# Two gate/up groups of each FFN as seven block products, interleaved with plain groups, and weights in blocks of 2048 columns

## The chip, the core and the metric

The kernel runs on one core of one Trainium2 chip. The metric is the device time of one execution in microseconds (us). TensorE (PE) multiplies, VectorE (DVE) and ScalarE (ACT) do the elementwise work, GpSimd (POOL) takes the powers in the norms, and SyncE (SP) issues the DMA transfers.

## The reference: what is computed

A two-layer decoder trunk over 256 tokens of width 1024. Each layer is FFN, mixer, FFN, so that there are four FFNs of width 2816; the mixers are a causal pooling and a dilated window attention. Every sublayer has an RMS norm on its input and one on its output. The part that the change is about:

```python
def swiglu(h, w_gate, w_up, w_down):
    return (jax.nn.silu(h @ w_gate) * (h @ w_up)) @ w_down
...
f = swiglu(rms_norm(h, g[0]), ffn_w_gate[layer, 0], ffn_w_up[layer, 0], ffn_w_down[layer, 0])
h = h + 0.5 * rms_norm(f, g[1])
```

## The kernel before, in words

The 256 tokens are two halves `i` of 128. A norm gives the activations, and `transposed` turns them with PE transposes into `aT`, as a rounded part (`aT[:, 0]`) and a rest (`aT[:, 1]`). The weights are treated the same way. `load_unit` (L83) loads a unit of 128x1024 fp32 (512 KB) into `raw` (four buffers) on SP's queue; ACT casts it to its rounded part (L92), DVE subtracts that from the unit for the rest (L93), and both stand in `hl` (eight buffers of one unit). Each product of a weight with an activation is three matmuls: rounded x rounded, rounded activation x rest of the weight, rest of the activation x rounded weight (`proj_mm` L106, `row_mm` L121). So ACT's cast has to be there for the first matmul with a unit, and DVE's subtraction for the second.

In an FFN (`ffn` L211) the 2816 hidden columns are five groups of 512 (`c` = 0 to 4) and one of 256 that holds gate and up beside each other (NG). A group's gate is 4 units, and so is its up; each unit serves both token halves. One group is 2 (gate, up) x 2 (halves) x 8 (blocks of 128 of the width) x 3 = 96 matmuls with 512 columns; an FFN has 5 x 96 + 48 = 528 of them. `gate` (L216) takes the silu on ACT, `up` (L221) multiplies on DVE, and `turn` (L226) transposes a half's product (four PE transposes, one ACT cast, one DVE subtraction) into `h2`, which the down projection reads: 22 units, 12 matmuls each. The last six units of the down projection (`TAIL`) are held back, so that half 0 is completed first: its post-norm, residual, next pre-norm and transposes (`Bound`, L306) run beside the last 36 matmuls of half 1. In the next FFN half 0 then has 48 matmuls (8 units of group 0) to be done while half 1 goes through the same norms.

Nobody writes out the order on the engines: a scheduler puts the instructions of each engine in a row when the kernel is built, by the order of the program and the buffers. Each engine then works its row strictly in that order, and so does SP's queue. Two things in the order matter below: a transfer into a buffer can be issued only when the last reader of that buffer is done, and whatever stands behind a waiting instruction on its engine waits too.

Of the kernel before, what the change touches and what calls it, by code (L numbers as in the profile page):

```python
# [11 lines left out]
F32 = mybir.dt.float32  # L12
F32R = mybir.dt.float32r
# [6 lines left out]
P = 128  # L20
S = 256
# [6 lines left out]
TAIL = 6  # L28
WARM = 64
CAST = 1024  # L30
# [17 lines left out]
def trunk_kernel(ctx: ExitStack, tc: tile.TileContext, x, pos, gains, pscale, ws, wq, invf, amask, pmat, icnt, out):  # L48
# [6 lines left out]
    s8p = ctx.enter_context(tc.tile_pool(name="s8p", bufs=6))  # L55
# [25 lines left out]
    unit_no = [0]  # L81
    last = {}

    def load_unit():
        u = unit_no[0]
        unit_no[0] += 1
        raw = rawp.tile([P, 1024], F32, tag="raw", name=f"raw{u}")
        last["dma"] = nc.sync.dma_start(raw, ws[u])
        hl = hlp.tile([P, 2, 1024], F32R, tag="hl", name=f"hl{u}")
        for c in range(0, 1024, CAST):  # L90
            w = slice(c, c + CAST)
            nc.scalar.copy(hl[:, 0, w], raw[:, w])  # L92
            last["dve"] = nc.vector.tensor_sub(hl[:, 1, w], raw[:, w], hl[:, 0, w])  # L93
        return hl

    def load_q_unit(u):
        raw = rawp.tile([P, 1024], F32, tag="raw", name=f"rawq{u}")
        nc.sync.dma_start(raw[:, :768], wq[u])
        hl = hlp.tile([P, 2, 1024], F32R, tag="hl", name=f"hlq{u}")
        nc.scalar.copy(hl[:, 0, :768], raw[:, :768])  # L100
        nc.vector.tensor_sub(hl[:, 1, :768], raw[:, :768], hl[:, 0, :768])
        return hl
# [72 lines left out]
    def transposed(i, src, dst, name):  # L175

        for b in range(2):
# [6 lines left out]
            nc.vector.tensor_sub(d[:, 1], tp, d[:, 0])  # L184

# [25 lines left out]
    def ffn(n, aT, boundary, middle=None):  # L211

        h2 = [s8p.tile([P, 2, 4, S], F32R, tag="s8", name=f"h2_{n}_{c}") for c in range(NG + 1)]
        act, prod = {}, {}

        def gate(c, i, g):  # L216
            w = g.shape[-1]
            act[c, i] = sc2.tile([P, 512], F32, tag="w2", name=f"s_{n}_{c}{i}")
            nc.scalar.activation(act[c, i][:, :w], g, AF.Silu)

        def up(c, i, u):  # L221
            w = u.shape[-1]
            prod[c, i] = sc2.tile([P, 512], F32, tag="w2", name=f"m_{n}_{c}{i}")
            nc.vector.tensor_mul(prod[c, i][:, :w], u, act[c, i][:, :w])
# [10 lines left out]
        def both(ps, units, c=None):  # L235

            for q in range(4):
                for i in range(2):
                    proj_mm(ps[i], aT, i, units, 512, only=q)
                if c is not None and q < 2:  # L240
                    turn(c, q)

        units = [load_unit() for _ in range(8 - len(first_units))]
        units, first_units[:] = first_units + units, []
# [11 lines left out]
        for c in range(1, NG):  # L256
            units = [load_unit() for _ in range(4)]
            ps = [gup.tile([P, 512], F32, tag="gu", name=f"g_{n}_{c}{i}") for i in range(2)]
            both(ps, units, c - 1)
            for i in range(2):  # L260
                gate(c, i, ps[i])
            units = [load_unit() for _ in range(4)]
            ps = acc_pair(f"u{n}{c}")
            both(ps, units)
            for i in range(2):
                up(c, i, ps[i])
            if c == 2 and middle is not None:
                middle()
        units = [load_unit() for _ in range(4)]
        ps = [gup.tile([P, 512], F32, tag="gu", name=f"g_{n}_{NG}{i}") for i in range(2)]  # L270
        both(ps, units, NG - 1)
        for i in range(2):
            gate(NG, i, ps[i][:, 0:256])
            up(NG, i, ps[i][:, 256:512])

# [7 lines left out]
        for c in range(NF - TAIL):  # L283
            u = load_unit()
            down(c, 0, u)
            down(c, 1, u)
# [477 lines left out]
```

## Time and profile before

| what | value |
|---|---|
| median of 3 runs | 992.54 us (991.7 to 993.55) |
| profiled execution, its own time | 995.63 us |
| its span, first to last instruction | 993.7 us |
| mean granted TensorE clock | 0.992 |
| PE busy | 975.3 us (98%) |
| DVE busy | 575.0 us (58%) |
| ACT busy | 484.4 us (49%) |
| DMA, over the span | 180.38 MB, mean 182 GB/s |

Terms are made against the profiled execution (995.63 us), which is 3.09 us above the median and 1.9 us longer than its span. In rows of groups, the last fields are the busy time in us, the mean duration in ns, and the idle time of the engine ahead of the group with what ended it. A busy PE may be waiting inside: the rate of PE is read from the starts of its instructions.

### The profile page before, as it was taken

The numbers are of one execution on the slowest core, as the hardware profiler recorded it, in microseconds if no ns is written. First come the engines' busy times: TensorE is split into PE (matmuls) and PEld (weight loads), VectorE is DVE, ScalarE is ACT, GpSimd is POOL, SyncE is SP. The second block draws the span as 40 slices with busy tenths as digits, with TensorE's granted clock in tenths as the row PEclk, the third lists the DMA queues.
The fourth block names the chain that finished last, engine by engine and source line by source line (L and its number), as shares of the span: only waits on it lengthen the run. The fifth ranks groups of instructions, "written<-read, shape, count | busy, mean of one in ns | idle before, by whom it ended". The sixth has DMA issues, their size and how long they took to land.

```text
span 993.7 us, 12240 instructions
## 1 busy us (share of the span) xinstructions
PE 975.3 (98%) x4664; PEld 810.1 (82%) x4664; DVE 575.0 (58%) x725; ACT 484.4 (49%) x660; POOL 23.2 (2%) x34
## 2 busy tenths in 40 slices
PE   7999999999999999999999999999999999999997
PEld 6888888878788888877888888788898888888886
DVE  5665554578765555447665554685556466555542
ACT  5644443365564444346554443554455565444431
POOL 0000000010100000000000000100000000000000
PEclk8999999999999999999999999999999899999999
DMA  6855655666465575535755756474533137556531
GB/s 224 292 185 188 228 186 189 203 193 213 145 218 185 190 233 180 191 127 174 263 188 171 231 179 197 150 244 154 152 124 128 44 100 260 191 181 203 188 127 42
DMA packets 53722, 180.38 MB, mean 182 GB/s; under 512 B 7265, under 2 KB 7265, under 8 KB 53665
## 3 DMA queue, kind: packets, MB, share of 16 engines
q1 hardware_dynamic: 53584, 179.35, 55.4%
q8 instruction: 36, 0.59, 0.2%
q0 software_dynamic: 80, 0.26, 0.1%
q14 instruction: 22, 0.17, 0.1%
HBM read 178.54 MB, written 1.05 MB: 181 GB/s over the span
## 4 chain that ended last, share of the span: by engine, by line
PE 88%; DVE 4%; issue 3%; ACT 2%; POOL 2%; DMA 1%; SPq 0%; POOLq 0%; DVEq 0%; ACTq 0%
PE g L105 22%; PE acc_d L105 21%; PE acc_u L105 19%; PE acc_b L105 7%; PE vp L105 3%; PE qp L105 3%; PE kp L105 3%; PE htp L230 2%; PE ob L105 1%; PE acc_w L105 1%; PE acc_o L105 1%; DVE h L171 1%; DVE hl L93 1%; ACT hl L92 1%; PE sc L105 1%
## 5 line engine op out<-in xcount | busy, mean ns | idle before, releaser
L93 DVE TENSOR_TENSOR hl<-raw,hl 128x1024 fp32r<-128x1024 f32 x310 | 378.5, 1224 | 298.8 <-ACT hl L92 296.7
L92 ACT CAST hl<-raw 128x1024 fp32r<-128x1024 f32 x310 | 325.5, 1051 | 338.5 <-PE acc_d L105 101.1
L105 PE MATMUL acc_d<-hl,h 128*128 128x512 f32 x1056 | 242.9, 390 | 0.0
L105 PEld LDWEIGHTS acc_d<-hl,h 128*128 128x128 f32 x1056 | 197.4, 188 | 40.7
L105 PE MATMUL g<-hl,aT_m 128*128 128x512 f32 x480 | 116.1, 394 | 0.0
L105 PEld LDWEIGHTS g<-hl,aT_m 128*128 128x128 f32 x480 | 88.6, 188 | 17.8
L105 PE MATMUL acc_u<-hl,aT_m 128*128 128x512 f32 x384 | 88.3, 389 | 0.0
L105 PEld LDWEIGHTS acc_u<-hl,aT_m 128*128 128x128 f32 x384 | 72.1, 188 | 15.0
L105 PE MATMUL acc_u<-hl,aT_f 128*128 128x512 f32 x288 | 67.2, 390 | 0.0
L105 PEld LDWEIGHTS acc_u<-hl,aT_f 128*128 128x128 f32 x288 | 53.8, 188 | 11.5 <-DVE aT_f L184 0.5
L105 PE MATMUL g<-hl,aT_f 128*128 128x512 f32 x240 | 58.7, 395 | 0.0
L105 PE MATMUL g<-hl,aT_x 128*128 128x512 f32 x240 | 58.1, 394 | 0.0
L105 PEld LDWEIGHTS g<-hl,aT_x 128*128 128x128 f32 x240 | 44.3, 188 | 8.9
L105 PEld LDWEIGHTS g<-hl,aT_f 128*128 128x128 f32 x240 | 44.2, 188 | 8.7
L105 PE MATMUL acc_b<-hl,aT_m 128*128 128x512 f32 x192 | 45.3, 392 | 0.1
L105 PE MATMUL acc_u<-hl,aT_x 128*128 128x512 f32 x192 | 44.2, 389 | 0.0
L105 PEld LDWEIGHTS acc_u<-hl,aT_x 128*128 128x128 f32 x192 | 36.0, 188 | 7.5
L105 PEld LDWEIGHTS acc_b<-hl,aT_m 128*128 128x128 f32 x192 | 35.7, 188 | 7.8 <-DVE aT_m L184 0.5
L105 PE MATMUL qp<-hlq,aT_f 128*128 128x384 f32 x192 | 39.1, 346 | 0.0
L105 PE MATMUL kp<-hl,aT_hk 128*128 128x512 f32 x144 | 34.5, 394 | 0.0
L105 PEld LDWEIGHTS qp<-hlq,aT_f 128*128 128x128 f32 x192 | 32.7, 188 | 0.4
L105 PE MATMUL vp<-hl,aT_hk 128*128 128x512 f32 x144 | 33.1, 390 | 0.0
(158 smaller groups left out, 831.3 us busy)
## 6 DMA issues: line engine op xcount, KB each, us to landing
raw<-in_ws SPq DMA_DIRECT2D x310, 512.0 KB, 3.5
rawq<-in_wq SPq DMA_DIRECT2D x16, 384.0 KB, 3.6
gain_post<-in_gains SPq DMA_DIRECT2D x14, 256.0 KB, 4.6
gain_pre<-in_gains SPq DMA_DIRECT2D x12, 256.0 KB, 5.6
rawpm<-in_pmat SPq DMA_DIRECT2D x2, 512.0 KB, 4.7
out_dram<-h SPq DMA_DIRECT2D x4, 256.0 KB, 2.1
h<-in_x SPq DMA_DIRECT2D x2, 256.0 KB, 3.0
h<-in_x SPq DMA_DIRECT2D x1, 512.0 KB, 8.5
```

Source lines behind the costliest of these rows:

```text
L92: nc.scalar.copy(hl[:, 0, w], raw[:, w])
L93: last["dve"] = nc.vector.tensor_sub(hl[:, 1, w], raw[:, w], hl[:, 0, w])
L105: nc.tensor.matmul(o, l, r, start=start, stop=stop)
L171: nc.vector.scalar_tensor_tensor(h[i][:, c], y[:, c], rs, h[i][:, c], op0=ALU.mult, op1=ALU.add)
L230: nc.tensor.transpose(tp[:, k], prod[c, i][:, k * P : (k + 1) * P], ident)
```

## The change

Groups 1 and 2 of an FFN become one `pair`, and so do groups 3 and 4. In a pair, the first group's gate and up are computed together. The activations, by token half and half of the width, are a 2x2 matrix A of blocks of 128x512. The weights are a 2x2 matrix of blocks of 512x512: X and W are the gate's columns in the first and the second half of the width, Y and Z the up's. Instead of eight products of a block of A with a block of weights, 12 matmuls each, there are seven: with X, X+Y, X+Y+Z, Z, Y+Z, W and X+Y+Z+W as weights, and with four sums of blocks of A, `S`, that `Sums` makes once after the norm (three ACT copies, four DVE sums, four ACT casts and four DVE subtractions of 128x512). The pair's second group is computed as before, its blocks placed between the seven products. So a pair has 84 + 96 = 180 matmuls instead of 192.

The weights come in blocks of 128x2048 (1 MB, two units). X and Y have buffers of their own (`xyp`, two), every other block goes through `rawp` (now three), and the halves through `hlp` (now three blocks, six units). The sums of weights are made in place by DVE (`add`); as each sum is a new weight, it is cast and subtracted anew: 7 + 4 wide casts and subtractions in a pair instead of 16 narrow ones (of the size of 8 wide ones), and 4 wide adds. X+Y+Z+W needs W. In `rawp`'s turn of three, W is the third block after Z, so it is loaded into Z's buffer. The norm of K and V moves from the middle of the third FFN (`middle`) to just ahead of its down projection (`late`).

The core of the diff:

```diff
-    rawp = ctx.enter_context(tc.tile_pool(name="rawp", bufs=4))
-    hlp = ctx.enter_context(tc.tile_pool(name="hlp", bufs=8))
+    rawp = ctx.enter_context(tc.tile_pool(name="rawp", bufs=3))
+    xyp = ctx.enter_context(tc.tile_pool(name="xyp", bufs=2))
+    hlp = ctx.enter_context(tc.tile_pool(name="hlp", bufs=3))
...
+    def load_raw(parts=1, pool=rawp, tag="raw"):
...
+        raw = pool.tile([P, 2, 1024], F32, tag=tag, name=f"{tag}{b}")
+        flat = raw.rearrange("p u n -> p (u n)")
+        for k in range(parts):
+            w = slice(k * (2048 // parts), (k + 1) * (2048 // parts))
+            last["dma"] = nc.sync.dma_start(flat[:, w], ws[b, :, w])
+        return raw
+
+    def halves(raw, parts=1, n=1024):
+        hl = hlp.tile([P, 2, 2, 1024], F32R, tag="hl", name="hl")
+        for k in range(parts):
+            u = slice(k * (2 // parts), (k + 1) * (2 // parts))
+            nc.scalar.copy(hl[:, 0, u, :n], raw[:, u, :n])
+            last["dve"] = nc.vector.tensor_sub(hl[:, 1, u, :n], raw[:, u, :n], hl[:, 0, u, :n])
+        return [hl[:, :, j] for j in range(2)]
...
+    class Sums:
...
+        def add_half(self, i, b, tp):
+            a = self.a
+            if (i, b) != (1, 1):
+                a[i, b] = self.tmp(f"{i}{b}")
+                nc.scalar.copy(a[i, b], tp)
+            if (i, b) == (1, 0):
+                s3 = self.tmp("s")
+                nc.vector.tensor_sub(s3, a[0, 0], tp)
+                self.parts(2, s3)
+            if (i, b) == (1, 1):
+                nc.vector.tensor_sub(a[1, 0], tp, a[1, 0])
+                self.parts(0, a[1, 0])
...
+        def parts(self, k, src):
+            nc.scalar.copy(self.out[:, k, 0], src)
+            nc.vector.tensor_sub(self.out[:, k, 1], src, self.out[:, k, 0])
...
+        def add(dst, src, k):
...
+                nc.vector.tensor_add(dst, dst, src)
+
+        def pair(c, turns):
+            x, y = [load_raw(1, xyp, "xy") for _ in range(2)]
+            z = load_raw()
+            px = bank()
+            product(px, plain(0, 0), halves(x), True)
+            p1 = temp("p1")
+            nc.scalar.copy(p1, px)
+            add(x, y, 0)
+            py = bank()
+            product(py, summed(0), halves(x), True)
+            p5 = temp("p5")
+            nc.scalar.copy(p5, py)
+            turns[0]()
+            g = [gup.tile([P, 512], F32, tag="gu", name=f"g_{n}_{c}{i}") for i in range(2)]
+            us = load_units(2)
+            both(g, us + us, (0, 1))
+            add(x, z, 1)
+            product(px, summed(1), halves(x), False)
+            u1 = temp("u1")
+            nc.scalar.copy(u1, px)
+            turns[1]()
+            us = load_units(2)
+            both(g, us + us, (2, 3))
+            for i in range(2):
+                gate(c + 1, i, g[i])
+            product(py, summed(3), halves(z), False)
+            c01 = temp("c01")
+            nc.vector.scalar_tensor_tensor(c01, py, -1.0, u1, op0=ALU.mult, op1=ALU.subtract)
+            add(y, z, 2)
+            product(px, summed(2), halves(y), False)
+            c11 = temp("c11")
+            nc.vector.scalar_tensor_tensor(c11, px, -1.0, p5, op0=ALU.mult, op1=ALU.subtract)
+            w = load_raw()
+            pz = bank()
+            product(pz, plain(0, 1), halves(w), True)
+            nc.vector.tensor_add(p1, pz, p1)
+            gate(c, 0, p1)
+            up(c, 0, c01)
+            add(x, w, 3)
+            product(px, plain(1, 1), halves(x), False)
...
+            us = load_units(2)
+            both(g, us + us, (0, 1))
+            turn(c, 0)
+            us = load_units(2)
+            both(g, us + us, (2, 3))
...
-        for c in range(1, NG):
-            units = [load_unit() for _ in range(4)]
...
+        pair(1, [lambda: turn(0, 0), lambda: turn(0, 1)])
...
+        pair(3, [turns12, lambda: turn(2, 1)])
...
-    ffn(2, aT, go, kv_input)
+    ffn(2, prev.aT, prev.sums, go, None, kv_input)
```

**DVE in the second FFN, the first group or pair after group 0.** Before, DVE's row is made of narrow subtractions (L93) for one unit each, with the multiplications and turns between them; `hl96` to `hl99` are the four units of group 1's up, `hl100` and `hl101` the first two of group 2's gate, and `h2_1_0` is group 0's turn:

```order
L93 TENSOR_TENSOR hl96_2415<-raw96_2413,hl96_2415 128x1024 [waits DMAHW3_49,Activation_49]
L93 TENSOR_TENSOR hl97_2420<-raw97_2418,hl97_2420 128x1024 [waits DMAHW4_49,Activation_49]
L224 TENSOR_TENSOR m_1_01_2323<-acc_b111_2220,s_1_01_2321 128x512 [waits PE_49]
L93 TENSOR_TENSOR hl98_2425<-raw98_2423,hl98_2425 128x1024 [waits DMAHW5_49,Activation_49]
L93 TENSOR_TENSOR hl99_2430<-raw99_2428,hl99_2430 128x1024 [waits DMAHW6_49,Activation_49]
L93 TENSOR_TENSOR hl100_2489<-raw100_2487,hl100_2489 128x1024 [waits DMAHW7_49,Activation_49]
L233 TENSOR_TENSOR h2_1_0_2171<-htp_1_00_2359,h2_1_0_2171 128x4x128 [waits Activation_49]
L93 TENSOR_TENSOR hl101_2494<-raw101_2492,hl101_2494 128x1024 [waits DMAHW0_49,Activation_49]
L233 TENSOR_TENSOR h2_1_0_2171<-htp_1_01_2378,h2_1_0_2171 128x4x128 [waits Activation_49]
```

After, in the same place: `xy46` is X and its sums, `xy47` is Y and Y+Z, `raw48` is Z, `raw49` and `raw50` are blocks of the plain group, `raw51` is W; L103 is the wide subtraction and L324 the wide add.

```order
L103 TENSOR_TENSOR hl_2193<-xy46_2167,hl_2193 128x2048 [waits Activation_49]
L289 TENSOR_TENSOR h2_1_0_2033<-htp_1_00_2210,h2_1_0_2033 128x4x128 [waits Activation_49]
L103 TENSOR_TENSOR hl_2221<-raw49_2219,hl_2221 128x2048 [waits DMAHW6_49]
L324 TENSOR_TENSOR xy46_2167<-xy46_2167,raw48_2171 128x2048 [waits DVE_49]
L289 TENSOR_TENSOR h2_1_0_2033<-htp_1_01_2266,h2_1_0_2033 128x4x128 [waits Activation_49]
L103 TENSOR_TENSOR hl_2249<-xy46_2167,hl_2249 128x2048 [waits Activation_49]
L103 TENSOR_TENSOR hl_2275<-raw50_2273,hl_2275 128x2048 [waits DMAHW7_49,PE_49,Activation_49]
L103 TENSOR_TENSOR hl_2306<-raw48_2171,hl_2306 128x2048 [waits Activation_49]
L324 TENSOR_TENSOR xy46_2167<-xy46_2167,raw51_2341 128x2048 [waits DMAHW0_49,DVE_49]
L103 TENSOR_TENSOR hl_2324<-xy47_2169,hl_2324 128x2048 [waits PE_49,Activation_49]
L103 TENSOR_TENSOR hl_2344<-raw51_2341,hl_2344 128x2048 [waits PE_49,Activation_49]
L354 SCALAR_TENSOR_TENSOR c01_1_2321<-st1_2192,u1_1_2264 128x512 [waits PE_49]
```

The add of W (`xy46_2167<-xy46_2167,raw51_2341`) now stands between the subtraction for Z and that for Y+Z (`hl_2324`), and it waits for a transfer.

**SP's queue in the same place.** Before, every load waits for the unit that was read four loads earlier:

```order
L88 DMA raw96_2413<-in_ws 128x1024 [waits DMAHW7_49,DVE_49]
L88 DMA raw97_2418<-in_ws 128x1024 [waits DMAHW0_49,DVE_49]
L88 DMA raw98_2423<-in_ws 128x1024 [waits DMAHW1_49,DVE_49]
L88 DMA raw99_2428<-in_ws 128x1024 [waits DMAHW2_49,DVE_49]
L88 DMA raw100_2487<-in_ws 128x1024 [waits DMAHW3_49,DVE_49]
L88 DMA raw101_2492<-in_ws 128x1024 [waits DMAHW4_49,DVE_49]
L88 DMA raw102_2497<-in_ws 128x1024 [waits DMAHW5_49,DVE_49]
```

After, `raw51` (W) waits for DVE, the last reader of Z, and the loads behind it stand in the same queue; `xy54` (the next pair's X) waits for X's buffer, which is in use until the last of the seven products has its halves.

```order
L94 DMA raw48_2171<-in_ws 128x2048 [waits DMAHW2_49,DVE_49]
L94 DMA raw49_2219<-in_ws 128x2048 [waits DMAHW3_49,DVE_49]
L94 DMA raw50_2273<-in_ws 128x2048 [waits DMAHW4_49,DVE_49]
L94 DMA raw51_2341<-in_ws 128x2048 [waits DMAHW6_49,DVE_49,Activation_49]
L94 DMA raw52_2386<-in_ws 128x2048 [waits DMAHW7_49,DVE_49]
L94 DMA raw53_2422<-in_ws 128x2048 [waits DMAHW5_49,DVE_49]
L94 DMA xy54_2455<-in_ws 128x2048 [waits DVE_49]
L94 DMA raw56_2459<-in_ws 128x2048 [waits DMAHW0_49,DVE_49]
L94 DMA xy55_2457<-in_ws 128x2048 [waits DVE_49]
```

So W's transfer can be issued only when DVE has subtracted Z.

**ACT between the pooling and the second FFN.** `jk_pm010`, `jk_pm011` are the squares for half 1's post-norm, `n_m00` is half 0's last norm step, `aT_m0` the casts of half 0's transposes. Before:

```order
L92 CAST hl88_2199<-raw88_2197 128x1024 [waits DMAHW3_49,PE_49]
L197 ACTIVATE n_m00_2074<-n_m00_2074,rs_qm00_2072 128x512 [waits Pool_49]
L92 CAST hl89_2204<-raw89_2202 128x1024 [waits DMAHW4_49,PE_49]
L183 CAST aT_m0_1649<-tp_m000_2079 128x4x128 [waits PE_49]
L183 CAST aT_m0_1649<-tp_m001_2086 128x4x128 [waits PE_49]
L92 CAST hl90_2209<-raw90_2207 128x1024 [waits DMAHW5_49]
L152 ACTIVATE jk_pm010_2130,ss_pm01_2129<-acc_w10_1949 128x512 [waits PE_49,Activation_49]
L92 CAST hl91_2214<-raw91_2212 128x1024 [waits DMAHW6_49,PE_49]
L152 ACTIVATE jk_pm011_2132,ss_pm01_2129<-acc_w11_1950 128x512 [waits Activation_49]
```

After:

```order
L102 CAST hl_2041<-raw42_2039 128x2048 [waits DMAHW1_49,PE_49]
L165 ACTIVATE jk_qm001_1911,ss_qm00_1908<-h0_100 128x512 [waits DVE_49,Activation_49]
L102 CAST hl_2046<-raw43_2044 128x2048 [waits DMAHW2_49,PE_49]
L249 ACTIVATE n_m00_1917<-n_m00_1917,rs_qm00_1915 128x512 [waits Pool_49]
L165 ACTIVATE jk_pm010_1977,ss_pm01_1976<-acc_w10_1812 128x512 [waits PE_49,Activation_49]
L102 CAST hl_2051<-raw44_2049 128x2048 [waits DMAHW3_49,PE_49]
L165 ACTIVATE jk_pm011_1979,ss_pm01_1976<-acc_w11_1813 128x512 [waits Activation_49]
L196 CAST aT_m0_1538<-tp_m000_1922 128x4x128 [waits PE_49]
L196 CAST aT_m0_1538<-tp_m001_1929 128x4x128 [waits PE_49]
```

The casts between the norm's steps are twice as wide, and the casts of `aT_m0`, for which PE's first matmuls of the FFN wait, now stand behind both squares and a wide cast (`hl_2051`) that itself waits for the end of the tail.

More of the change, by code (lines that the diff above doesn't have):

```diff
@@ new lines, in product @@
+        def product(ps, a, units, start):
+            for k in range(4):
+                u = units[k // 2][:, :, (k % 2) * 512 : (k % 2) * 512 + 512]
+                for n, (z, v) in enumerate(((0, 0), (0, 1), (1, 0))):
+                    nc.tensor.matmul(
+                        ps,
+                        a(z, k),
+                        u[:, v],
+                        start=start and k == 0 and n == 0,
+                        stop=k == 3 and n == 2,
+                        skip_group_check=not start,
+                    )
@@ L511, in trunk_kernel @@
     for g in range(3):
[L512 removed]
+        units = load_units(4)
         for i in range(2):
@@ L622, in trunk_kernel @@
             values(1, 1)
-    units = [load_unit() for _ in range(4)]
+    units = load_units(4)
     scores(1, 2, gup, "gu")
```

227 lines of the change are left out of this document (135 added, 92 removed).

## The prediction

> **What bounds the kernel now.** I read the page first: busy times, the chain that ended last, the costliest groups.
>
> ```profile
> span 993.7 us, 12240 instructions
> PE 975.3 (98%) x4664; PEld 810.1 (82%) x4664; DVE 575.0 (58%) x725; ACT 484.4 (49%) x660; POOL 23.2 (2%) x34
> PE 88%; DVE 4%; issue 3%; ACT 2%; POOL 2%; DMA 1%; SPq 0%; POOLq 0%; DVEq 0%; ACTq 0%
> L93 DVE TENSOR_TENSOR hl<-raw,hl 128x1024 fp32r<-128x1024 f32 x310 | 378.5, 1224 | 298.8 <-ACT hl L92 296.7
> L92 ACT CAST hl<-raw 128x1024 fp32r<-128x1024 f32 x310 | 325.5, 1051 | 338.5 <-PE acc_d L105 101.1
> ```
>
> The chain is PE for 88% of the span. DVE and ACT wait for PE (338.5 us of ACT ahead of its casts), not PE for them. So matmuls taken away are time gained, as long as DVE and ACT keep ahead. The chain in order of time gives PE's rate, here from one gate group to the next:
>
> ```profile
> 84.58 2.72 PE g L105 x12
> 87.74 2.78 PE g L105 x12
> 90.95 5.46 PE g L105 x24
> 96.41 10.88 PE acc_u L105 x48
> 107.29 2.72 PE g L105 x12
> ```
>
> Twelve matmuls take 2.72 us (0.2267 us each); 87.74 - 84.58 - 2.72 = 0.44 us is a turn's four transposes; a group takes 107.29 - 84.58 = 22.71 us, which is 96 x 0.2267 + 2 x 0.44 with 0.07 left. PE does not wait there at all. The busy times by stretch show what room the others have in such a group:
>
> ```profile
> core 0: us, PE busy (x) PEld busy (x) DVE busy (x) ACT busy (x) POOL busy (x), PEclk, DMA share, GB/s
> 307.30:330.00 22.70, 22.70 (x105) 18.80 (x104) 12.20 (x13) 10.48 (x12) 0.00 (x0) 1.00 0.56 186
> ```
>
> DVE is busy 12.2 of 22.7 us. Boundaries between sublayers are nearly as tight: the timeline of the one into the third FFN has, on PE,
>
> ```profile
> 447.40 1.06 PE L181 MATMUL tp_f<-ident,n_f 128*128 128x128 f32 x8 [0.71 <-DVE n_f L195]
> 448.22 1.40 PE L105 MATMUL acc_d<-hl,h 128*128 128x512 f32 x5
> 449.46 8.65 PE L105 MATMUL acc_b<-hl,aT_f 128*128 128x512 f32 x36
> 458.49 1.06 PE L181 MATMUL tp_f<-ident,n_f 128*128 128x128 f32 x8 [0.37 <-DVE n_f L195]
> 459.31 13.87 PE L105 MATMUL acc_b<-hl,aT_f 128*128 128x512 f32 x60
> ```
>
> Half 0's transposes fall inside the down projection's tail, 36 matmuls of the new FFN cover half 1's norms, and PE waits 0.71 + 0.37 us.
>
> **The gain.** A pair drops 12 matmuls, eight pairs 96: 96 x 0.2267 = 21.8 us of PE work.
>
> **Durations of the wide operations.** No row has 2048 columns; I extend the two sizes of the same form.
>
> ```profile
> L101 DVE TENSOR_TENSOR hlq<-rawq,hlq 128x768 fp32r<-128x768 f32 x16 | 15.3, 958 | 16.0 <-ACT hlq L100 15.8
> L100 ACT CAST hlq<-rawq 128x768 fp32r<-128x768 f32 x16 | 13.4, 837 | 11.1 <-PE qp L105 7.4 <-PE vp L105 3.6
> L233 DVE TENSOR_TENSOR h<-htp,h 128x512 fp32r<-128x512 f32 x40 | 27.3, 684 | 0.0
> 62.99 1.23 DVE L93 TENSOR_TENSOR hl<-raw,hl 128x1024 fp32r<-128x1024 f32 x1 [0.30 <-ACT hl L92]
> 64.13 0.16 DVE L354 CAST posf<-pi 128x2 f32<-128x2 int32 x1
> ```
>
> DVE: 1224 - 958 = 266 ns for 256 columns, so 1224 + 4 x 266 = 2.29 us; the next one starts 0.09 us before an end (64.13 against 62.99 + 1.23), so 2.2 us each in a row, narrow ones 0.6. ACT: 1051 + 4 x 214 = 1.91 us. The wide add has the same form (two fp32 operands from SBUF), so 2.2 us too; its bounds are the 690 ns that one-operand casts of 1024 columns take (1.3 us for 2048) and twice the narrow subtraction (2.45 us).
>
> **A pair on DVE.** 11 wide subtractions and 4 wide adds are 15 x 2.2 = 33 us; 4 turns, 4 multiplications and 3 combinations are 11 x 0.6 = 6.6; together 39.6 us, where PE has 180 x 0.2267 + 4 x 0.44 = 42.6 us. Before it was 24.4 of 45.4 us. DVE goes from half idle to 93%, so its waits, which were free, now reach PE. I follow the second FFN's first pair, whose DVE row is shown with the change, with time 0 at PE's first matmul with X.
>
> DVE does the adds X+Y and Y+Z while group 0 ends and starts the subtraction for X+Y at 2.2. Subtraction, turn, subtraction, add of Z, turn: 2.2 + 3 x 2.2 + 2 x 0.6 = 10.1. ACT can cast X+Y+Z only after that add (9.5), to 11.5; then three subtractions (X+Y+Z, plain block, Z) end at 18.2. PE, with 0.4 + 0.3 + 0.75 us lost on these, begins Z at 21.4 and ends it at 24.1.
>
> Now W. Its load goes into Z's buffer, so it is issued at 18.3. What a load of 1 MB takes, from issue to landing, no row shows:
>
> ```profile
> raw<-in_ws SPq DMA_DIRECT2D x310, 512.0 KB, 3.5
> 820.00:825.00 5.00, 5.00 (x24) 4.14 (x23) 3.49 (x4) 2.97 (x4) 0.00 (x0) 1.00 0.89 324
> SPq L88 <- DVE hl L93: 651.9, 276, 23.1
> ```
>
> Half of it takes 3.5 us and loads flow at 324 GB/s, so the second half adds 0.524 MB / 324 GB/s = 1.6: 5.1 us. Bounds: 3.5 (no more than half of it) and 7.0 (twice). The last row says that SP was waiting for DVE's reads before, too: 651.9 us, but nobody waited for SP, since eight halves stood ready. Now W lands at 23.4; the add of W, for which DVE stands still since 18.2, ends at 25.8; the subtraction for Y+Z, queued behind it, at 28.0. PE has needed that since 24.3: it waits 3.7 us. (The wait is the landing time less 1.4 us: 2.1 at 3.5, 5.6 at 7.0.)
>
> The next pair's X has the same trouble: its buffer is free after the subtraction for X+Y+Z+W (33.0), it lands at 38.2, and group 1's product, whose multiplication stands behind that subtraction on DVE, reaches PE's turn 1.5 us late. In the second pair the same steps give 1.7 us at X+Y and 2.8 at Y+Z. Sum for two pairs: 360 x 0.2267 + 7 x 0.44 = 84.7 us of work, 6.9 + 4.7 us of waits, 96.3 us, against 4 x 22.71 = 90.8; the eighth turn falls behind them, 0.4. So +5.9 us in an FFN, **+23.8 us** in four (with 3.5 us for a load +1.1 and +4.4; with 7.0, +12.2 and +49).
>
> By the Trainium skill's "DMA: Bandwidth & Descriptors" (section on the anatomy of one DMA) a transfer takes about 2.0 us plus its bytes at 436 GB/s, which would be 4.4 us for 1 MB, an estimate of that page for another issuing path; the four FFNs would then lose some 15 instead of 24 us. The trace's 3.5 us for 0.5 MB lies 0.3 above the page's 3.2, and I keep the rows.
>
> **The boundaries.** From pooling into the second FFN, with 0 at the end of half 0's tail and 8.2 us of half 1's tail to go:
>
> ```profile
> 441.37 1.41 DVE L171 SCALAR_TENSOR_TENSOR h<-y_f,rs_pf,h 128x512 f32<-128x512 f32 x2
> 445.27 1.46 POOL L156 TENSOR_TENSOR rs_qf<-ms_qf,nhalf 128x1 f32<-128x1 f32 x1 [3.94 <-DVE ms_qf L154]
> ```
>
> Before, such a chain from the residual to the power took 445.27 - 441.37 = 3.9 us with a narrow cast and a narrow subtraction inside. Now they are wide (+0.9, +1.1), and the transposes come at 10.5, no longer inside the tail: 2.35 us of waiting, and their own 0.9. ACT then has two squares and a wide cast ahead of the casts of `aT` (2.7), DVE a wide subtraction ahead of the rests (1.0). Of four blocks only three are in `hlp`, so 25 instead of 36 matmuls stand ahead of half 1's transposes, and half 1's norms are late by the same wide casts (0.8); the fourth block waits for a buffer (0.4). Together 7.3 + 0.9 - 0.9 of before: +7.3 us. The same count for the third FFN, where `aT`'s casts stand earlier, gives +5.5. The others I estimate from these two by what their rows hold: attention into the fourth FFN +4 (one wide cast in the chain), first FFN into pooling +4.5 (no sums), third FFN into K and V +1.5 (another `aT` is ready). **+22.8 us**, bounds 10 (only the widths counted) and 30.
>
> **The rest.** `Sums` costs DVE 8 x 0.6 and ACT 7 x 0.58 us, under group 0's 21.8 us of matmuls: nothing, beyond the fourth block's wait above. If that cover were short, X would start later, up to 5 us each. The norm of K and V now stands ahead of the down projection's first blocks on DVE (about 5 us of narrow work and two powers): +2. Rope tables in the first FFN's second pair: +1.5. K, V and Q with three blocks instead of eight units, with DVE's rope between the subtractions: +3. The start, with the sums: +1. **+7.5 us**, bounds 0 and 15. Down projections: 24 matmuls (5.4 us) per block against 2.2 and 1.9: nothing.
>
> Sum: 23.8 + 22.8 + 7.5 = 54.1; 995.6 + 54.1 = 1049.7 in a profiled execution, and 3.1 less as a median: **1047 us**.
>
> **Rivals.**
>
> *Small waits* (15%). A load of 1 MB lands in 3.5 us and the boundaries cost only the widths: 4.4 + 10 + 5 = 19, so 1012 us. For it: half blocks showed 3.1 to 3.5 us. Against it: bytes take time.
>
> *PE's clock falls in the new waits* (22%). The trace has one such place besides the start, in attention, where small work and waits leave PE thinly used:
>
> ```profile
> 785.00:790.00 5.00, 4.27 (x21) 3.44 (x20) 3.54 (x10) 3.60 (x9) 0.86 (x1) 0.66 0.00 0
> 790.00:793.00 3.00, 3.00 (x12) 2.71 (x13) 0.00 (x0) 0.59 (x1) 0.00 (x0) 0.50 0.00 0
> ```
>
> The granted clock is 0.66 and then 0.50: 5 x 0.34 + 3 x 0.5 = 3.2 us lost. The new waits at Y+Z (3.7 us) and around half 0's transposes (2.35 + 2.7 with only transposes between) may do this at four boundaries and four pairs: 8 x 3.2 = 26 us, so 1073 us; at half of them 1060. Against it: the boundary above kept 1.00 with waits of 0.71 and 0.37. The Trainium skill's "TensorE: Matmul & The Clock Gate" (Part 1, the HAM clock gate) says that an idle window of about 3.4 us halves the clock; by that rule the first pairs' wait of 3.7 could be enough, the second pairs' 2.8 not, and no wait of before was that long except at the start.
>
> *Faster* (9%). The wide operations run at the one-operand rate of 690 ns per 1024 columns (1.3 us for 2048). DVE's 15 in a pair would fall from 33 to 20 us, the waits on it vanish, and the pairs keep their gain: 360 matmuls and turns, 84.8 us for two pairs, 6 less than before, -24 in all; with boundaries at 10 and the rest at 4 it ends at 983 us. It decides when a wide subtraction or add takes under 1.7 us (waits then under the 2.7 us that a pair gains). Against it: both rows of the same form grow by 266 ns per 256 columns, with no sign of a faster rate.
>
> *The change hardly acts* would need 192 matmuls in a pair; its row on PE has 180.
>
> **How the numbers follow.** Forecast as worked out 53%, clock 22%, small waits 15%, faster 9%, near no change 1%. About 0.2% (2 us) is what a measurement of this kernel can tell from none. The range goes from the small-waits case (1012, taken as 1010) to the clock case's upper end (1073) with the bounds of the loads added in part (1080). Faster 9%, same 1%, slower 90%.
>
> **What would show it.** In the profile after: PE's matmuls fall by 96; L103's wide subtraction near 2.29 us, the wide cast near 1.91, the wide add like the subtraction; DVE's wait for the DMA of `raw` ahead of the add, some 5 us, eight times; PE waiting for `hl` of Y+Z 3 to 4 us in first pairs; DVE near 90% busy in pairs; `raw` landing in about 5.1 us; in the second FFN some 31 us from the end of the tail to X instead of the 23.5 (459.31 + 60 x 0.2267 - 449.46) that the third FFN took before. I am wrong if PE stays without waits in the pairs, or if the wide operations are much below 2.2 us.

## The result and the profile after

The changed kernel takes **1014.74 us** (median of 4 runs, 1013.72 to 1015.7) against 992.48 us: ratio 1.0223, 95% interval 1.0206 to 1.0241. That is 22.3 us slower. The forecast was 1047 us: the direction was right, the size was not. The first lines of the page and the groups that the prediction speaks of (last fields: busy time, mean ns, idle time ahead and what ended it; for a transfer, KB and us to landing):

```profile
span 1011.8 us, 11346 instructions
PE 975.8 (96%) x4568; PEld 800.0 (79%) x4568; DVE 706.8 (70%) x675; ACT 531.6 (53%) x591; POOL 23.8 (2%) x34
...
L103 DVE TENSOR_TENSOR hl<-xy,hl 128x2048 fp32r<-128x2048 f32 x40 | 91.4, 2286 | 10.1 <-ACT hl L102 9.9
L102 ACT CAST hl<-xy 128x2048 fp32r<-128x2048 f32 x40 | 76.7, 1918 | 39.7 <-DVE xy L324 30.8
...
L324 DVE TENSOR_TENSOR xy<-xy,raw 128x2048 f32<-128x2048 f32 x24 | 54.8, 2285 | 0.1
...
raw<-in_ws SPq DMA_DIRECT2D x137, 1024.0 KB, 4.8
```

PE has 96 matmuls less (4664 to 4568). The wide operations last what was extended from the narrow ones: 2.29 us (forecast 2.29) and 1.92 (1.91). But ahead of the 24 adds that read `raw`, the eight adds of W among them, DVE was idle for 0.1 us in all, where the forecast had some 5 us eight times. So the pairs are the first place to look. Here are both pairs of the second FFN by busy time (columns as in the prediction: length, busy time of PE, PEld, DVE, ACT and POOL, granted clock, DMA share, GB/s), in the kernel before (its groups 1 to 4) and then in the changed one:

```profile
284.56:375.43 90.87, 90.87 (x418) 75.21 (x416) 50.80 (x50) 42.96 (x49) 0.00 (x0) 1.00 0.64 211
```

```profile
292.74:379.36 86.62, 86.10 (x390) 69.76 (x389) 78.96 (x51) 54.22 (x44) 0.00 (x0) 1.00 0.58 213
```

DVE is busy for 78.96 us, as forecast (2 x 39.6), and yet PE hardly waits: 4.25 us are gained where 5.5 were to be lost. From the starts of PE's instructions the difference splits like this (X is the first product of a pair, in the kernel before the first gate matmul of group 1; in the fourth FFN, where the end of group 0 stands between X's matmuls, X is counted from that end):

| stretch | before, us | after, us | difference | forecast |
|---|---|---|---|---|
| the two pairs, four FFNs | 365.4 | 346.9 | -18.4 | +23.8, with the eighth turn; +1.5 for the rope tables |
| gate and up of NG, with the eighth turn | 47.3 | 50.2 | +2.9 | in the line above |
| pooling, first to last matmul | 57.3 | 60.0 | +2.7 | +4.5 |
| pooling to X of the second FFN | 23.5 | 32.7 | +9.2 | +7.3 |
| third FFN's group 0 | 23.6 | 27.3 | +3.8 | +5.5 |
| end of Q to X of the fourth FFN | 59.4 | 76.3 | +16.9 | +4, and part of +3 |
| K, V, Q | 125.1 | 124.4 | -0.7 | +1.5, and part of +3 |
| down projections and start | | | +1.6 | +3 |

The sum is +18.0, the difference of the spans 18.1 us. So there are two errors of opposite sign: the pairs are 39 us better than forecast, attention 10 us or more worse. The first two lines also hold the move of the norm of K and V: before, it stood among the third FFN's groups 1 to 4 (92.8 us there, 90.9 in each of the other FFNs), and now some 0.8 us of its transposes stands in the line of NG. Without that move the pairs differ by -16.5 us and are some 38 us better than forecast.

**Why W does not wait.** DVE and SP in the second FFN's first pair (X starts at 292.74):

```profile
299.88 2.29 DVE L324 TENSOR_TENSOR xy<-xy,raw 128x2048 f32<-128x2048 f32 x1
...
306.40 4.49 DVE L103 TENSOR_TENSOR hl<-raw,hl 128x2048 fp32r<-128x2048 f32 x2
310.81 2.28 DVE L324 TENSOR_TENSOR xy<-xy,raw 128x2048 f32<-128x2048 f32 x1
313.01 2.28 DVE L103 TENSOR_TENSOR hl<-xy,hl 128x2048 fp32r<-128x2048 f32 x1
```

```profile
300.02 0.33 SPq L94 DMA_DIRECT2D raw<-in_ws  x1
...
308.72 0.33 SPq L94 DMA_DIRECT2D raw<-in_ws  x1
...
310.92 0.33 SPq L94 DMA_DIRECT2D raw<-in_ws  x1
...
315.32 0.33 SPq L94 DMA_DIRECT2D xy<-in_ws  x1
```

Z's subtraction is the second of the two that end at 310.89, 18.15 us after X: the forecast had 18.2. The add of W follows at once, at 310.81, because W's load was not the one issued at 310.92 but the one at 300.02, right after the subtraction for the plain group's first block (`raw49`). **W goes into that block's buffer, not into Z's.** The rows on record said so: the load of `raw51` waits for `DMAHW6`, which is the transfer that the readers of `raw49` waited for. The statement ahead of the prediction, that W is loaded into Z's buffer, is wrong. So is the one on the next pair's X (`xy54`), the load issued at 315.32: it waits for Y's buffer, not for X's. It goes out right after the subtraction for Y+Z, which ends at 315.29, 22.6 us after X, where the forecast had 33.0. In both cases the load got the buffer of its pool that came free first, not the one whose turn it was.

**The clock in attention.** Two stretches of the changed kernel, behind the last Q matmul:

```profile
769.43:774.70 5.27, 4.11 (x31) 3.41 (x31) 5.27 (x14) 3.16 (x7) 0.00 (x0) 0.98 0.46 146
774.70:788.85 14.15, 14.15 (x52) 11.37 (x51) 6.64 (x19) 5.64 (x14) 0.00 (x0) 0.50 0.27 94
```

In the first, DVE is busy throughout: a wide subtraction (769.00, 2.29 us) stands ahead of the last rope, and PE is short of work for 1.16 us. Then the granted clock is 0.50 up to 795 us, some 20 us. In the kernel before, the clock fell only later in attention, behind the first matmuls with w_o: 0.66 and 0.50 from 785 to 793 us, in the rows that the prediction shows.

**Theories.** A (width): the pairs keep most of their gain; what is lost is lost outside them, where a wide cast or subtraction stands ahead of short operations that PE waits for, and where the clock falls in such waits. B (buffers): the loss comes from three blocks in place of eight units. C: the forecast. D: the sums of activations make the loss at the boundaries.

### The profile page after: what moved, and what is told of

Read it like the earlier page. It is cut to its first block, busy times and chain, and to the rows that moved or that the text cites. A ratio compares the mean times of both kernels' runs of the same rounds, so it can differ in the third digit from the quotient of the medians.

```text
span 1011.8 us, 11346 instructions
## 1 busy us (share of the span) xinstructions
PE 975.8 (96%) x4568; PEld 800.0 (79%) x4568; DVE 706.8 (70%) x675; ACT 531.6 (53%) x591; POOL 23.8 (2%) x34
## 5 line engine op out<-in xcount | busy, mean ns | idle before, releaser
L103 DVE TENSOR_TENSOR hl<-raw,hl 128x2048 fp32r<-128x2048 f32 (+1 forms) x141 | 318.0, 2259 | 177.7 <-ACT hl L102 177.2
L102 ACT CAST hl<-raw 128x2048 fp32r<-128x2048 f32 (+1 forms) x141 | 265.3, 1885 | 189.5 <-PE acc_d L118 106.3
L103 DVE TENSOR_TENSOR hl<-xy,hl 128x2048 fp32r<-128x2048 f32 x40 | 91.4, 2286 | 10.1 <-ACT hl L102 9.9
L102 ACT CAST hl<-xy 128x2048 fp32r<-128x2048 f32 x40 | 76.7, 1918 | 39.7 <-DVE xy L324 30.8
L118 PE MATMUL g<-hl,aT_m 128*128 128x512 f32 x288 | 70.5, 396 | 1.0 <-ACT hl L102 1.0
L118 PEld LDWEIGHTS g<-hl,aT_m 128*128 128x128 f32 x288 | 52.8, 188 | 13.2 <-ACT hl L102 1.8
L324 DVE TENSOR_TENSOR xy<-xy,raw 128x2048 f32<-128x2048 f32 x24 | 54.8, 2285 | 0.1
L305 PE MATMUL st<-hl,S_m 128*128 128x512 f32 x192 | 47.2, 393 | 0.6 <-DVE hl L103 0.6
L118 PE MATMUL u<-hl,aT_m 128*128 128x512 f32 x192 | 45.9, 391 | 0.0
L118 PE MATMUL qp<-hl,aT_f 128*128 128x384 f32 x192 | 39.7, 347 | 0.0
L118 PEld LDWEIGHTS qp<-hl,aT_f 128*128 128x128 f32 x192 | 32.7, 188 | 0.6
```

The source lines that it names most:

```text
L102: nc.scalar.copy(hl[:, 0, u, :n], raw[:, u, :n])
L103: last["dve"] = nc.vector.tensor_sub(hl[:, 1, u, :n], raw[:, u, :n], hl[:, 0, u, :n])
L118: nc.tensor.matmul(o, l, r, start=start, stop=stop)
L305: nc.tensor.matmul(ps, a(z, k), u[:, v], start=start and k == 0 and n == 0, stop=k == 3 and n == 2, skip_group_check=not start,)
L324: nc.vector.tensor_add(dst, dst, src)
```

## The experiments

Each time stands with its ratio to the kernel before, measured beside it on the same chip (992.7 to 993.7 us).

**1. Narrow operations outside the pairs** (`halves` in two steps, the load still 1 MB). Q's blocks, which are loaded in another place, stay wide.

```diff
-        return [u for _ in range(n // 2) for u in halves(load_raw(parts), parts)]
+        return [u for _ in range(n // 2) for u in halves(load_raw(parts), max(parts, cut))]
```

> The kernel after, with every block outside the pairs cast and subtracted in two narrow operations (128x1024) instead of one wide one; loads of 1 MB, buffers and pairs as they are. Theory A (width): the changed kernel loses some 34 us outside the pairs (9 between pooling and the second FFN, 16 in attention and its boundary, 9 elsewhere), because wide casts and subtractions stand ahead of short operations that PE waits for, and because the granted clock falls in these waits; the pairs keep 16 to 18 us of their gain. Then most of the 34 us goes: 980 to 992 us, with the mean clock back near 0.99. Theory B (buffers): the loss comes from three blocks where there were eight units; then narrow operations bring no more than 4 us: 1010 to 1015. Theory C (the forecast): the wait for W in the pairs is the largest term; then this changes the boundaries alone, and the pairs still show 3 to 4 us of waiting each.

993.88 us, ratio 1.0015 (1.0001 to 1.0029). 20.9 us come back, with the same three blocks in `hlp`: A holds, B as the whole cause does not; 2 us above A's range would leave a part to B, or to what else the blocks bring (the 1 MB loads, the late norm). Where the time went, between pooling and the second FFN, in the changed kernel:

```profile
259.84 2.29 DVE L103 TENSOR_TENSOR hl<-raw,hl 128x2048 fp32r<-128x2048 f32 x1
...
259.86 2.68 POOL L169 TENSOR_TENSOR rs_qm<-ms_qm,nhalf 128x1 f32<-128x1 f32 x1 [5.88 <-DVE ms_qm L167]
...
263.11 1.97 PE L194 MATMUL tp_m<-ident,n_m 128*128 128x128 f32 x8 [3.10 <-DVE n_m L247]
...
266.77 8.86 PE L118 MATMUL acc_b<-hl,aT_m 128*128 128x512 f32 x25 [1.69 <-ACT aT_m L196]
```

and in this one:

```profile
255.09 0.55 POOL L170 TENSOR_TENSOR rs_qm<-ms_qm,nhalf 128x1 f32<-128x1 f32 x1 [3.96 <-DVE ms_qm L168]
...
256.21 1.09 PE L195 MATMUL tp_m<-ident,n_m 128*128 128x128 f32 x8 [0.64 <-DVE n_m L248]
...
259.21 3.11 PE L119 MATMUL acc_b<-hl,aT_m 128*128 128x512 f32 x13
```

The waits of 3.10 and 1.69 us become 0.64 and none, and half 0's transposes are back inside the tail.

**2. Narrow operations for w_o alone**, the two blocks that stand ahead of the last rope.

```diff
-    units = load_units(4)
+    units = load_units(4, 1, 2)
     scores(1, 2, gup, "gu")
```

> The kernel after, with only the two blocks of the attention's output projection (w_o) cast and subtracted in narrow operations. Theory A: 9 us of the attention's loss hang on one wide subtraction that stands ahead of the last rope on DVE (769.00, 2.29 us): without it PE does not run dry, and the clock does not stay at 0.5 for 20 us. So 1004 to 1007 us, with the clock of 775 to 795 us near 1.00. Theory B: no change, 1014 to 1015. A rival within A: the clock falls a little later all the same, as it did in the kernel before (0.66 and 0.50 for 8 us): then 1008 to 1011.

1005.25 us, ratio 1.0125 (1.0103 to 1.0147), 9.5 us better, as A expected. From the end of Q to the first matmul with w_o it is 11.7 us, in the changed kernel 19.4. But the granted clock is 1.00 there in this profile, and most of the difference goes with that: the profiles of experiments 3 to 6 keep the wide subtraction ahead of the last rope, also show 1.00, and take 12.8 us; experiment 1, whose w_o is narrow too, takes 12.7 at 1.00. That it is the wide subtraction that brings the fall of the clock is not shown.

**3. Wide blocks without pairs.** `pair` is replaced by two plain groups, the sums are gone, the weights lie in that order.

```diff
-        pair(1, [lambda: turn(0, 0), lambda: turn(0, 1)])
...
-        pair(3, [turns12, lambda: turn(2, 1)])
+        for c in range(1, NG):
+            group(c, [lambda i=i: turn(c - 1, i) for i in range(2)])
```

> Blocks of 2048 columns and the buffers of the kernel after (three for blocks, three for halves), but all groups computed as in the kernel before: no products of sums, no sums of activations or weights, 24 more matmuls an FFN. It leaves nothing of the result out. Theory A: the wide blocks alone cost what the changed kernel loses outside the pairs: 992.5 + 34 less what the sums of activations do there (0 to 8 us) = 1018 to 1027 us. Theory D (the sums of activations make the loss at the boundaries): near the kernel before, 993 to 1003. The forecast's terms for boundaries and rest would give 992.5 + 30 = 1023, so this run does not tell A from it there, but it tells both from D.

1018.17 us, ratio 1.0258 (1.024 to 1.0276): A's range. The blocks cost 25 us without any sum, so D as the whole cause falls. In these 25 us the width, the 1 MB loads, the fewer buffers and the late norm are together.

**4. W in Z's buffer, as the forecast had it.** Z and W have a pool of one buffer, `rawp` has two, and the blocks outside take both pools in turn. The add of W is put ahead of the subtraction for Y+Z.

```diff
-            z = load_raw()
+            z = load_raw(1, zwp, "zw")
...
-            product(px, summed(2), halves(y), False)
+            w = load_raw(1, zwp, "zw")
+            with tc.issue_after(add(x, w, 3).ins):
+                hy = halves(y)
+            product(px, summed(2), hy, False)
```

> The kernel after with what the forecast assumed of W: Z and W share one buffer, so W's load can only be issued after the subtraction for Z, and the add of W is put ahead of the subtraction for Y+Z on DVE. If the forecast's price for this is right (2.8 to 3.7 us at Y+Z in each pair with a landing time of 5.1 us, 2.5 to 3.4 with the 4.8 us that the profile after shows, and a later X for the next pair), the time rises by 18 to 24 us, to 1033 to 1039. Rival: PE and DVE have slack that hides most of it, under 6 us, 1015 to 1021.

1057.01 us, ratio 1.0642 (1.0618 to 1.0666): 42.3 us more than the changed kernel, where I had expected 18 to 24. The place that the forecast worked out (X at 307.19):

```profile
325.35 0.33 SPq L95 DMA_DIRECT2D zw<-in_ws  x1
...
331.58 0.69 DVE L362 SCALAR_TENSOR_TENSOR c<-st,u 128x512 f32<-128x512 f32 x1 [6.26 <-PE st L313]
332.19 2.28 DVE L332 TENSOR_TENSOR xy<-xy,zw 128x2048 f32<-128x2048 f32 x1
...
336.73 4.38 PE L313 MATMUL st<-hl,S_m 128*128 128x512 f32 x11 [2.83 <-DVE hl L104]
```

```profile
307.19:405.33 98.14, 90.42 (x392) 72.46 (x391) 77.07 (x51) 54.55 (x45) 0.00 (x0) 0.97 0.49 182
```

W's load is issued 18.16 us after X (forecast 18.3). PE waits 1.70 us at W (333.40) and 2.83 at Y+Z, 4.5 together, where the forecast had 3.7 at Y+Z; eleven matmuls then last 4.38 us, since the clock falls. DVE's 6.26 us here ended with PE's product with Z, since the combination (`c`) stands ahead of the add; for the transfer of W itself DVE waited 14.4 us in the eight adds of W together, where the forecast had some 5 us each. Two pairs take 98.14 us here and 98.8 to 101.4 in the other FFNs; the forecast had 96.3 without any fall of the clock, which costs 0.03 x 98 = 2.9 us of these 98.14. So the price was about right, for a wait that the changed kernel does not have: the 42.3 us are close to the 39 by which the pairs came out better than forecast. Here the clock falls in all eight pairs.

**5. W in Z's buffer, DVE's order left to the scheduler** (Z and W share a buffer as in 4, but W's load and its add stand where they were).

> W and Z share one buffer, as in the run that forced the order (1057.0 us), but DVE's order is left to the scheduler, which now puts the add of W behind the subtraction for Y+Z. If it is the add's place in DVE's row that makes a late W dear, this is much cheaper than 1057: W lands 4.8 us after Z's subtraction (18.3 + 4.8 = 23.1 after X's first matmul), PE needs W's halves at about 27 and X+Y+Z+W's at about 30, so 0 to 2 us a pair: 1015 to 1030 us. If a late W costs the same in any order, 1050 us or more.

1027.89 us, ratio 1.0348 (1.0327 to 1.037). The add now stands behind the subtraction for Y+Z. Two pairs take 90.8 to 95.6 us: 2.8 us a pair over the changed kernel, not 0 to 2, but less than half of the 6.3 in 4. So both count: where the add stands in DVE's row, and how late the load is.

**6. Idle filled between pooling and the second FFN.** 80 matmuls of zeros are added.

```diff
+            fill("mm", FILL[0])
+            fill("tp_m00", FILL[1])
         go(i, f[i])
```

> The kernel after, with 80 idle-filling matmuls of zeros on PE (bf16, 128x128, into a bank that nobody reads) in the two waits between pooling and the second FFN: 54 ahead of half 0's transposes (a wait of 3.1 us), 26 ahead of the first matmuls with its aT (1.69 us). They take no wait away. If the halved clock there (0.5 from 262 to 272 us, 4.9 us lost) is the answer to an idle PE, the clock stays at 1.00 and the time falls by 4 to 5 us, to 1009.5 to 1011. If the clock falls for another reason, or the lost time is the waits alone, no change (1014 to 1015.5) or the fill's own overhang (up to 1017).

1009.63 us, ratio 1.0165 (1.0125 to 1.0205), but the single times are 1004.52, 1009.46, 1009.79 and 1014.57. Two rows of the fastest: the first is pooling's end to X, the second the end of Q to the first matmul with w_o.

```profile
260.80:293.38 32.58, 29.09 (x192) 23.94 (x191) 25.05 (x29) 17.54 (x27) 3.63 (x3) 1.00 0.36 130
769.97:782.74 12.77, 11.64 (x79) 9.62 (x79) 11.22 (x28) 8.24 (x18) 0.00 (x0) 1.00 0.44 166
```

In the changed kernel the first reads

```profile
260.01:292.74 32.73, 27.94 (x114) 22.22 (x114) 24.98 (x29) 17.45 (x27) 3.62 (x3) 0.84 0.35 129
```

So the fill keeps the clock (0.84 to 1.00), and the stretch is as long as before: 32.58 against 32.73 us. But the fill also changed the scheduler's order on PE. Up to half 1's transposes (`tp_m` below) the changed kernel has

```profile
266.77 8.86 PE L118 MATMUL acc_b<-hl,aT_m 128*128 128x512 f32 x25 [1.69 <-ACT aT_m L196]
275.47 1.03 PE L194 MATMUL tp_m<-ident,n_m 128*128 128x128 f32 x8
```

and the filled one

```profile
269.42 4.15 PE L119 MATMUL acc_b<-hl,aT_m 128*128 128x512 f32 x17 [1.13 <-DVE aT_m L205]
274.75 1.06 PE L202 MATMUL tp_m<-ident,n_m 128*128 128x128 f32 x8 [1.18 <-DVE n_m L255]
```

With two matmuls at 267.56 it has 19 ahead of the transposes instead of 25; six (1.4 us) stand behind them now, and PE waits 1.18 us for half 1's norm. In the changed kernel PE does not wait there: at half the clock it comes 15.46 us after pooling's end, here after 13.95. **So the halved clock cost something there, though not the 4 to 5 us that I had given as my reason.** The profile of experiment 7, which has the changed kernel's order there and gets the full clock back some 2 us earlier, has the transposes after 14.26 us and X after 31.56, both 1.2 us sooner. What the full clock gained here was lost again by the order.

The gain came from attention, where nothing was changed: same order on ACT and DVE, same waits, but this time the clock stayed at 1.00 and it took 12.77 us, not 19.42. The stage is at an edge. Over whole executions the mean clock of the changed kernel was 0.979 in all four; here it was 0.994 in the fastest and 0.984 to 0.987 in the others.

**7. Idle filled in attention.**

```diff
+        for _ in range(FILL.get((i, hd), 0)):
+            nc.tensor.matmul(sc[:, 0:P], zeros, zeros, start=True, stop=True)
         mm(sc[:, 0:256], q[0][a, t], kT[0][a, pr, :], True, True)
```

> The kernel after, with 20 idle-filling matmuls of zeros (bf16, 128x128, into the bank that the next score matmuls then overwrite) in PE's wait of 0.85 us behind the last wide subtraction of attention: 14 ahead of the scores of half 1's head 2, 6 ahead of those of head 3. The orders on DVE and ACT stay as they are. The kernel after runs at half clock there from 775 to 795 us; in the profile with the filled pool gap the same order kept 1.00 and took 9.5 us less. If an idle PE brings the clock down, it now stays up in every run: 1004 to 1007 us, all runs within 3 us. If the fall there has another cause, 1013 to 1017, or runs of both kinds, 10 us apart.

1007.88 us (1004.49 to 1009.34), ratio 1.0142 (1.0119 to 1.0165). The runs lie 5 us apart where I expected 3, and reach 2 us above the expected range, but none is near 1014. The same two stretches as shown of the changed kernel:

```profile
768.46:773.70 5.24, 5.24 (x45) 4.14 (x45) 5.24 (x13) 2.81 (x5) 0.00 (x0) 1.00 0.42 138
773.70:782.06 8.36, 8.36 (x56) 6.84 (x55) 6.08 (x16) 5.45 (x15) 0.00 (x0) 1.00 0.45 166
```

More work on PE, and less time: 8.36 in place of 14.15 us for the second. From the end of Q to X of the fourth FFN the profile has 67.8 us, the one of experiment 6 66.8 and the changed kernel 76.3. So the fall of the clock is 7 to 8 us of the loss by the medians (1014.74 to 1007.88, or by the two ratios 0.0081 x 993), 8.5 to 9.5 by the profiles. That PE's idle time brings it down fits this, but is not shown: the profiles of experiments 3 to 6 kept 1.00 at this place without the fill. What makes the changed kernel fall in all its executions stays open. What parts the runs of 1004.5 and 1009.3 stays open.

**8. Wide blocks narrowed, without pairs** (3 with `halves(load_raw(parts), 2)`).

> The run with blocks but no pairs (1018.2 us), now with narrow casts and subtractions for every block. It says what width and what the smaller number of buffers cost in that kernel, and, beside the kernel with pairs and narrow operations outside them (993.9 us), what the pairs are worth. Theory A: width is the larger part, 1000 to 1008 us, and the pairs are worth 6 to 14 us net of the sums of activations. Rival 1 (buffers): it stays at 1012 to 1018 us. Rival 2 (the pairs' gain is eaten by the sums): 992 to 996 us, so that the pairs are worth nothing.

1005.55 us, ratio 1.0126 (1.0111 to 1.0141): narrow operations take back 12.6 us of the blocks' 25 (any change of the clock included), and the pairs, with wide operations inside them, are worth 1005.55 - 993.88 = 11.7 us.

**9. Narrow everywhere, halves in six buffers of a unit** in place of three of a block, the pairs included.

```diff
-    hlp = ctx.enter_context(tc.tile_pool(name="hlp", bufs=3))
+    hlp = ctx.enter_context(tc.tile_pool(name="hlp", bufs=6))
...
+            hl.append(hlp.tile([P, 2, 1024], F32R, tag="hl", name="hl"))
+            nc.scalar.copy(hl[u][:, 0, :n], raw[:, u, :n])
```

> Narrow casts and subtractions everywhere, inside the pairs too, and the halves in six buffers of one unit in place of three of a block (the same bytes), so that a unit's buffer comes free by itself. Theory A with buffers as its remainder: the kernel with narrow operations outside (993.9 us) still takes 5 us longer than the kernel before from attention to the last FFN's first pair, since two units are held for one; then 985 to 990 us. Rival: in the pairs DVE has 11 x 0.16 = 1.8 us more in 42.6 us of which 39.6 were taken; if that brings PE to wait for it, 8 pairs lose 1 us each or more: 998 to 1004 us.

**981.90 us** (981.78 to 985.01), ratio **0.9894** (0.9875 to 0.9912): faster than both kernels, and 12.0 us below 1.

```profile
281.83:367.81 85.98, 85.69 (x389) 70.23 (x388) 81.45 (x76) 57.87 (x68) 0.00 (x0) 1.00 0.60 222
...
755.09:765.38 10.29, 10.11 (x80) 8.11 (x79) 9.12 (x29) 7.20 (x19) 0.00 (x0) 1.00 0.52 181
```

DVE is busier in the pairs (81.45 us of 85.98, 95%), and they are no slower for it: 85.0 to 86.8 us against 86.6 to 86.9. The end of Q to w_o is back at 10.29 us (10.28 before). Narrow pairs and freer buffers came together here and are not told apart.

**10. The same with loads of 512 KB.**

> The fastest kernel so far (narrow operations, halves in six units: 981.9 us), with every block loaded by two transfers of 512 KB in place of one of 1 MB. A unit can then be cast when half of its block has landed, 1.3 us earlier (4.8 against 3.5 us). If the size of a transfer is part of what the wide blocks cost at the boundaries, 977 to 980.5 us; if loads stand ready there, no change, 981 to 984.

985.61 us, ratio 0.9921 (0.9904 to 0.9937): 3.7 us slower than 9, against my expectation. In the rows a half lands in 4.6 us (`raw`) and 5.8 (`xy`), a whole block in 4.8 and 5.1, but these medians mix first and second halves. By its trace the first half of a block lands 3.9 us after its issue, 0.9 earlier than a whole block (I had expected 1.3), and the second 5.4 us after the first one's issue, 0.6 later. Where the 3.7 us go stays open.

**11. Number 9 without pairs.**

> The same kernel (narrow operations, halves in six units, loads of 1 MB) without the pairs: all groups as in the kernel before, 96 more matmuls, no sums. It leaves nothing of the result out. It prices the seven products by themselves. By the pairs' windows (85.0 to 86.8 us against 90.85 in the kernel before) they are worth 4 x 4.9 = 20 us, less what the sums of activations cost at the boundaries: 993 to 1001 us. Rival: the sums and the orders that come with them cost most of it again, under 988 us.

999.33 us, ratio 1.0061 (1.0046 to 1.0076): the pairs are worth 17.4 of their 21.8 us here. Against 8, units in place of blocks bring 6.2 us. What is left, 5.7 us above the kernel before, is not told apart: loads of 1 MB, six units where there were eight, and the late norm. In the wide kernel the pairs are worth only 3.4 us (1018.17 - 1014.74), and much of the rest is lost in attention: from the end of Q to the end of group 0 it takes 76.3 us with pairs and 65.4 in experiment 3, whose profile shows a clock of 1.00 up to w_o.

## Why the prediction was wrong in size, point by point

- **Durations of the wide operations: right** (2.29 and 1.92 us; the add 2.285), and so DVE's load in a pair. A load of 1 MB took 4.8 us, between the 5.1 from the rows and the 4.4 that was estimated, for another issuing path, from the Trainium skill's "DMA: Bandwidth & Descriptors" (anatomy of one DMA).
- **The pairs' waits, +23.8 us: the step that failed.** "Its load goes into Z's buffer, so it is issued at 18.3" was an assumption about a pool, and the row that contradicts it was quoted. W is issued 7.3 us after X (300.02 - 292.74), lands before DVE needs it, and the term is -15.5 us (-18.4 and NG's +2.9). The next pair's X, priced at 1.5 and 1.7 us in the same term, goes into Y's buffer 22.6 us after X and not into X's at 33.0. Experiment 4 made the assumption on W true and found pairs of 98.1 to 101.4 us for the 96.3 forecast, and a kernel of 1057 us for the 1047. Two slips in the term's sum bear on nothing: 2.2 + 3 x 2.2 + 2 x 0.6 is 10.0, and the waits that are named add to 6.7 and 4.5 where 6.9 and 4.7 are summed.
- **Boundaries of pooling, second and third FFN: right in mechanism, close in sum.** +15.7 us measured, 17.3 forecast; experiment 1, with narrow operations, leaves 1.3, 1.3 and 1.0 of it, so the widths make most of it. Part of the second FFN's +9.2 is the halved clock, some 1.2 us, which the term did not hold. For the second FFN the chain from residual to power is as worked out (254.01 to 259.86, 5.85 us, for 3.9 + 0.9 + 1.1), but the power itself takes 2.68 us in place of 1.46.
- **Attention into the fourth FFN, +4: mis-sized.** Measured +16.9 (59.4 to 76.3). By the profiles some 9.5 us of it go with the clock (76.3 to 66.8 in experiment 6), 1.8 with the width (65.0 in experiment 1), 2.7 with blocks in place of units (62.4 in experiment 9) and 2.7 with the sums of activations (59.6 in experiment 11). I had looked at the boundary's norm chain, not at the w_o blocks ahead of the last rope.
- **The clock rival (22%)** named the right effect and the wrong places: the pairs kept 1.00, the pool boundary fell to 0.50 at a cost of at least 1.2 us (experiments 6 and 7), and attention fell and cost 7 to 9.5 us. Why it falls there stays open.
- **Rest, +7.5: measured about +1 to +2.** The late norm costs some 2 us in its new places and saves 1.9 among the third FFN's groups; the start is 0.8 us shorter.
- **"Faster" (9%)** asked for quicker wide operations. They stayed slow, and in a pair PE had no need of quicker ones.

## What to carry to other kernels

Look up which buffer a load really gets, from the semaphore that it waits for, before a wait is priced on it: wrong buffers for two loads were most of the 39 us by which this forecast missed the pairs. An elementwise operation made twice as wide may be free inside a dense stretch and dear where short operations queue behind it: the blocks, above all the width of their operations, and not the seven products, cost these 22 us. Narrow operations outside the pairs brought 20.9 us back, with the clock in attention among them; narrow operations everywhere in buffers of a unit turned a loss of 2.2% into a gain of 1.1%. What a halved clock costs is to be measured stage by stage. A few filling matmuls can tell it, but only if they leave the order as it was; those of experiment 6 did not.

## What the runs showed of the hardware

- **The clock can fall without any long wait.** In attention the longest single idle time was 0.85 us, 1.16 of 5.27 us together, and the stretch behind it ran at 0.50 in the changed kernel's profile and, with the same order and waits there, at 1.00 in experiment 6's: 76.3 and 66.8 us from the end of Q to X of the fourth FFN. The Trainium skill's "TensorE: Matmul & The Clock Gate" (Part 1, the HAM clock gate) names an idle window of some 3.4 us ahead of the half clock, and no wait here is as long; its remark that the window is free-running would fit the two executions, but no run here shows it.
- **A power on POOL waits for a subtraction on DVE.** It takes 0.55 us alone, 1.40 to 1.47 behind a narrow subtraction that began just ahead (before), 2.46 to 2.68 behind a wide one (after, three times). The Trainium skill's "SBUF — State Buffer" (two separate sides) says that the two share a port pair, which a DVE operation with two SBUF inputs holds for its whole length against a GpSimd operation that reads SBUF; the trace agrees.
